# A decoder layer on one core: second Strassen group of the down-projection reordered over two pairs, operand differences emitted earlier, and the last column sums split over two banks

## The chip, the cores and the metric

The kernel runs on one core of a Trainium2 chip. The metric is the device time of one execution in microseconds (us). The profile is of one execution; its own time stands beside its span in the table below. TensorE is called PE in the profile's rows, VectorE DVE, ScalarE ACT, GpSimd POOL, and SyncE, which issues most DMAs here, SP.

## The reference

One layer of a hybrid decoder over 1024 tokens of width 1024: a normalisation, two attention branches, a merge, and then a gated MLP with a short convolution. The change lies wholly in the last product and the final normalisation:

```python
def conv_ffn(xn, w_up, conv_w, conv_b, w_down):
    ...
    gate, val = jnp.split(c, 2, axis=-1)
    return (jax.nn.silu(gate) * val) @ w_down
...
    x = x + conv_ffn(xn, w_up[l], conv_w[l], conv_b[l], w_down[l])
return rmsnorm(x, norm_final_w)
```

`w_down` is 2816 x 1024. Everything is float32.

## The kernel before

Activations lie transposed: 128 channels on the partitions, 1024 tokens along the free axis, in two halves of 512. To keep float32 accuracy on a faster matmul type, each operand is split into a high part (a cast on ScalarE) and a low part (the operand less its high part, a subtraction on VectorE). A product of two operands is then three matmuls: high x high, high x low and low x high. For four blocks of 128 on the inner axis that makes 12 matmuls of 512 columns into one PSUM bank.

**The down-projection, `down()`.** The hidden axis has 22 blocks of 128 rows. The first six (`N1 = 6`) are multiplied plainly. The other sixteen are two groups of eight, and each group is multiplied by Strassen's scheme (in Winograd's form): a weight block row `m` (0 to 3) with row `m + 4` makes a **pair**, the two token halves are the other side, and a pair takes seven products instead of eight:

- P1 = A11 x B11, P2 = A12 x B21, P3 = S4 x B22, P4 = A22 x T4, P5 = S1 x T1, P6 = S2 x T2, P7 = S3 x T3.

A11 and A12 are the raw weight blocks of row `m`, A22 the second of row `m + 4`; S1 to S4 are sums and differences of weight blocks, made on GpSimd with four additions per pair. B11, B21, B22 are blocks of the activations; T1 to T4 are differences of them, made on VectorE by `diffs(k, ...)` with four subtractions for each of four inner blocks `k`.

The result accumulates in one tile `x3` of 8 x 1024 columns in SBUF: VectorE adds each finished bank to it (rows `x<-x,d` and `x<-x,y` in the profile; `d` and `y` are the two kinds of bank, four of each in `psD`).

**Order of the first group.** P1 and P2 of all four pairs come first; then the loop `for m, y in enumerate(ys)` (L1231) runs for each pair P5, P6, P3, P4, P7, that is 60 matmuls. Inside this loop `diffs(k, i)` is emitted four times (L1245, L1250): it makes the differences for the *second* group, each time tied behind one of VectorE's additions by `tc.issue_after`.

**Order of the second group.** The list `more` holds closures that split each activation operand (`prepare(n)` emits the next n). All of B11, B21, T4, T2, T3 and the four result boxes are emitted before the loop over the pairs (L1252); the rest during it. For each pair the loop (L1277) runs P1, P2, then P7 of the pair before (`seventh`), P4, P6. P5 and P3 of the second group come last for all pairs (`fifth`, `third`), because they finish the right half of the tokens, and the final normalisation follows behind them piece by piece. `evac` adds a bank to `x3`, squares the finished sum on ScalarE (L1261), adds the squares up, and multiplies by the norm's weight on ScalarE (L1265).

**Where weights come from.** `plan()` writes a list `wsrc`; `next_w(n)` calls `ahead(n)`, which takes entries from the list and issues loads, GpSimd sums and splits until `n` weight operands are queued. A "second" entry is one pair of the second group: `second_pair` (L138) loads both rows, makes the four sums on GpSimd (L148 to L151), stores S1 and S4 to DRAM (`sd`), and splits A11/A12, S2/S3 and A22. The buffers are few: three raw tiles (`raw`, RAW = 3), two high and two low tiles for A operands (`wh`, `wl`), two of each for S operands (`sh`, `sl`), two for the GpSimd sums (`c`). A cast into a `wh` tile waits until the matmuls that read the operand two before it are done.

**The scheduler.** Tile, the layer under the kernel, places the emitted instructions in one fixed order per engine; each engine then runs strictly in that order. SP's queue is a fixed order too.

**The end, `last_norm`** (L1336). For each piece of tokens `col_sums` (L214) multiplies the squares with a column of ones on PE, block of 128 tokens by block, all into one bank; `rstd_cols` (L221) scales on VectorE (L225) and takes the power on GpSimd (L227); `spread` transposes the result across partitions (L233), and L1361 multiplies and L1362 stores. The right half of the tokens is done in two pieces of 256; the second one ends the program.

Of the kernel before, what the change touches and what calls it, by code (L numbers as in the profile page):

```python
# [10 lines left out]
F32 = mybir.dt.float32  # L11
# [6 lines left out]
P = 128  # L18
D = 1024
# [25 lines left out]
class Trunk:  # L45
    def __init__(self, tc, ins, out):
        self.tc, self.nc = tc, tc.nc
        (self.xT, self.w_in, self.w_br, self.w_mix, self.w_up, self.w_dn,
         self.vecs_d, self.bias_d) = ins
        self.out = out  # L50
        self.uid = 0
        self.stores = []
        self.uw = self.w22 = self.behind = None
        self.pin, self.after = False, None
        self.hs, self.defer, self.late = {}, [], []
# [14 lines left out]
    def ahead(self, n):  # L70
        while len(self.wq) < n and self.wsrc and (self.wsrc[0][1] != "pair" or self.uw):
            src, nk, *eng = self.wsrc.pop(0)
            if nk == "sums":

                self.sums = self.split_pair(*self.sum_pair(src, True, "sl"), 1, 3)
            elif nk == "rest":
                self.sums["A22"] = self.load_w(src[1][:, 4:8], 4)
                self.wq.append(self.sums)
            elif nk == "second":
                self.wq.append(self.second_pair(src, *eng))  # L80
# [57 lines left out]
    def second_pair(self, src, m):  # L138

        nc = self.nc  # L140
        raws = []
        for x in src:
            raws.append(self.tl(self.wp, [P, 8, P], "raw", bufs=RAW))
            nc.sync.dma_start(raws[-1], x)
        g, v = (r.rearrange("p (k a) c -> p a k c", a=2) for r in raws)
        sa, sb = (self.tl(self.sfp[0], [P, 2, 4, P], self.sfp[1]) for _ in range(2))
        tt = nc.gpsimd.tensor_tensor
# [4 lines left out]
        nc.sync.dma_start(self.sd[m], sa.rearrange("p a k c -> p (a k) c"))  # L152
        ops = {}
        for pool, h, l, x, names in ((self.wp, "wh", "wl", g, ("A11", "A12")), (self.uw, "sh", "sl", sb, ("S2", "S3")), (self.wp, "wh", "wl", v[:, 1:2], ("A22",))):
            hi = self.tl(pool, [P, len(names), 4, P], h, F32R)
            lo = self.tl(pool, [P, len(names), 4, P], l, F32R)
            nc.scalar.copy(hi, x)
            nc.vector.tensor_tensor(lo, x, hi.bitcast(F32), ALU.subtract)
            for i, name in enumerate(names):
                ops[name] = hi[:, i], lo[:, i]  # L160
        return ops
# [59 lines left out]
    def rstd_cols(self, ssq_ps, n, width):  # L221
# [3 lines left out]
        nc.vector.tensor_scalar(ms[:, :n], ssq_ps[:, :n], 1.0 / width, EPS, ALU.mult, ALU.add)  # L225
# [52 lines left out]
    def plan(self):  # L278
# [28 lines left out]
        src += [((self.w_dn[m, :, N2:, :], self.w_dn[m + 4, :, N2:, :]), "second", m) for m in range(4)]  # L307
# [800 lines left out]
    def down(self):  # L1108

        nc, tc = self.nc, self.tc  # L1110
        with ExitStack() as ctx:
# [118 lines left out]
            for m, y in enumerate(ys):  # L1230
# [6 lines left out]
                tt(col(m, 1), col(m, 1), y, ALU.add)  # L1237
# [6 lines left out]
                if m in (1, 2):  # L1244
                    diffs(2 * m - 1, i)  # L1245
# [3 lines left out]
                if m < 2:  # L1249
                    diffs(2 * m, i)  # L1250
            prepare(24)
# [3 lines left out]
            def evac(ps, m, hf, a=0, b=H2, last=False):  # L1255
# [5 lines left out]
                nc.scalar.activation(sq, x, AF.Square)  # L1261
# [3 lines left out]
                nc.scalar.mul(x, x, self.vecs[:, C_NO + m:C_NO + m + 1])  # L1265
                return sq

            ys, ws = [], []

# [5 lines left out]
            for m in range(4):  # L1275
                w = self.next_w()
                ws.append(w)  # L1277
# [6 lines left out]
                if m:  # L1284
                    seventh(m - 1)
                ps = bank(0)
                self.product(ps, w["A22"], "2T4")
                tt(col(m + 4, 0), col(m + 4, 0), ps, ALU.subtract)
                self.product(y, w["S2"], "2T2", first=False, skip=True)
                tt(col(m, 1), col(m, 1), y, ALU.add)  # L1290
                prepare(4)
            seventh(3)
# [26 lines left out]
            for a, b in ((0, q), (q, H2)):  # L1319
# [4 lines left out]
                sqs = [box[1][:, a:b], third(2, ws[2], p[0], a, b, True)]  # L1324
                if not a:
                    step()
                sqs.append(third(3, ws[3], p[1], a, b, True))
# [8 lines left out]
    def last_norm(self, psD, sqs, x3, t0, a, b, pieces):  # L1336
# [4 lines left out]
        def sums():  # L1341
            ssq = self.tl(psD, [P, H2], "d")
            self.col_sums(ssq, sqs, n, 0)
# [85 lines left out]
```

## Time and profile before

| | |
|---|---|
| time, median of 3 runs | 1343.12 us (1343.10 to 1344.14) |
| the profiled execution's own time | 1343.35 us |
| its span | 1341.1 us |
| PE busy | 1321.7 us (99%) |
| VectorE busy | 1065.8 us (79%) |
| ScalarE busy | 621.7 us (46%) |
| GpSimd busy | 495.6 us (37%) |
| granted PE clock, mean | 0.995 |
| the first group's pairs (P5 to P7) | from 1190.08 us |
| the second group's first product | from 1244.90 us |
| the last large matmul | ends near 1330.2 us |

Rows of the timeline give the start, the duration, the engine, the line of the kernel, the operation, the output and inputs with their shapes, how many instructions were merged, and in brackets how long the engine had been idle and what ended the wait. A row's duration is a little longer than the distance to the next start where instructions overlap: a VectorE addition of 512 columns shows 0.68 but the next one starts 0.60 later, and matmuls of 512 columns start every 0.227 us while each shows 0.39. A row merged from several instructions gives the sum.

### The profile page before, as it was taken

The numbers are of one execution on the slowest core, as the hardware profiler recorded it, in microseconds if no ns is written. First come the engines' busy times: TensorE is split into PE (matmuls) and PEld (weight loads), VectorE is DVE, ScalarE is ACT, GpSimd is POOL, SyncE is SP. The second block draws the span as 40 slices with busy tenths as digits, with TensorE's granted clock in tenths as the row PEclk, the third lists the DMA queues.
The fourth block names the chain that finished last, engine by engine and source line by source line (L and its number), as shares of the span: only waits on it lengthen the run. The fifth ranks groups of instructions, "written<-read, shape, count | busy, mean of one in ns | idle before, by whom it ended". The sixth has DMA issues, their size and how long they took to land.

```text
span 1341.1 us, 17306 instructions
## 1 busy us (share of the span) xinstructions
PE 1321.7 (99%) x6264; PEld 1097.4 (82%) x6264; DVE 1065.8 (79%) x1603; ACT 621.7 (46%) x1019; POOL 495.6 (37%) x365
## 2 busy tenths in 40 slices
PE   7999999999999999999999999999999999999997
PEld 6888888888888778878888888888888888888787
DVE  8847775289889876465678999999999987869975
ACT  8432232276667665333454444334444434323443
POOL 0336552000102124641446555655556510224412
PEclk9999999999999999999999999999999999999998
DMA  6423443966553235334423222222222239562333
GB/s 258 148 104 150 149 157 141 254 174 188 143 138 130 93 121 200 138 110 157 141 96 108 65 93 90 83 81 77 95 79 90 75 116 330 202 246 71 113 115 126
DMA packets 63045, 182.64 MB, mean 136 GB/s; under 512 B 6896, under 2 KB 15216, under 8 KB 62960
## 3 DMA queue, kind: packets, MB, share of 16 engines
q1 hardware_dynamic: 51504, 164.13, 37.3%
q10 hardware_dynamic: 11456, 17.41, 3.6%
q8 instruction: 49, 0.80, 0.2%
q14 instruction: 36, 0.29, 0.1%
HBM read 130.66 MB, written 50.86 MB: 135 GB/s over the span
## 4 chain that ended last, share of the span: by engine, by line
PE 86%; DVE 5%; POOL 4%; DMA 2%; issue 2%; ACT 1%; POOLq 0%; SPq 0%; ACTq 0%; DVEq 0%
PE t L920 13%; PE t L919 13%; PE t L918 13%; PE g L210 3%; PE g L211 3%; PE g L212 3%; PE t L912 3%; PE sc L634 3%; PE y L1157 2%; PE d L1157 2%; PE sc L212 2%; PE sc L210 2%; PE sc L211 2%; DMA gr<-gd 2%; PE d L918 2%
## 5 line engine op out<-in xcount | busy, mean ns | idle before, releaser
L1087 ACT ACTIVATE c<-us,vecs 128x512 f32<-128x512 f32 x80 | 61.3, 781 | 132.3 <-POOL us L1081 128.3
L1089 DVE SCALAR_TENSOR_TENSOR c<-us,vecs,c 128x512 f32<-128x512 f32 x160 | 110.4, 747 | 8.6 <-ACT c L1087 8.5
L1081 POOL TENSOR_TENSOR us<-us,rstd 128x1024 f32<-128x1024 f32 x38 | 99.6, 2642 | 4.5 <-DVE us L467 2.4
L128 DVE TENSOR_TENSOR sl<-sf,sh 128x1024 fp32r<-128x1024 f32 x62 | 87.6, 1416 | 11.5 <-ACT sh L127 11.5
L127 ACT CAST sh<-sf 128x1024 fp32r<-128x1024 f32 x62 | 63.4, 1048 | 60.4 <-PE t L919 44.0
L177 DVE TENSOR_TENSOR wl<-raw,wh 128x1024 fp32r<-128x1024 f32 (+2 forms) x46 | 57.7, 1255 | 30.2 <-ACT wh L175 18.9
L128 DVE TENSOR_TENSOR wl<-raw,wh 128x1024 fp32r<-128x1024 f32 (+1 forms) x35 | 75.9, 2169 | 3.7 <-ACT wh L127 3.6
L103 POOL TENSOR_TENSOR sf<-rv 128x512 f32<-128x512 f32 x30 | 41.3, 1377 | 100.9 <-DVE sl L128 57.8
L175 ACT CAST wh<-raw 128x1024 fp32r<-128x1024 f32 (+2 forms) x46 | 46.0, 1001 | 62.6 <-PE sc L211 30.5
L210 PE MATMUL g<-xh,wh 128*128 128x512 f32 x176 | 70.7, 402 | 0.1
L212 PE MATMUL g<-xh,wl 128*128 128x512 f32 x176 | 70.4, 400 | 0.0
L211 PE MATMUL g<-xl,wh 128*128 128x512 f32 x176 | 70.3, 400 | 0.0
L108 POOL TENSOR_TENSOR sf<-raw,rv 128x512 f32<-128x512 f32 x30 | 40.7, 1356 | 65.4 <-DVE sl L128 65.4
L617 POOL MEMSET aT<- 128x128 f32 x32 | 6.1, 205 | 151.5 <-PE t L663 63.2
L638 DVE CUSTOM_DVE_ANT_0 L<-sc,bias 128x128 f32<-128x128 f32 (+7 forms) x64 | 47.7, 751 | 17.0 <-PE sc L634 13.7
L639 ACT ACTIVATE L<-L,sm 128x128 f32<-128x128 f32 (+7 forms) x64 | 49.6, 778 | 20.0 <-DVE sm L638 13.5
L792 POOL TENSOR_TENSOR gr<-gr,rstd 128x1024 f32<-128x1024 f32 x16 | 40.4, 2533 | 41.2 <-DMA gr<-gd 40.9
L1091 ACT ACTIVATE c<-c 128x512 f32<-128x512 f32 x40 | 24.0, 600 | 60.7 <-DVE c L1089 60.7
L128 DVE TENSOR_TENSOR wl<-rv,wh 128x512 fp32r<-128x512 f32 x30 | 49.2, 1640 | 3.5 <-ACT wh L127 3.5
L634 PE MATMUL sc<-u,u 128*128 128x512 f32 (+2 forms) x192 | 49.7, 358 | 0.0
L212 PE MATMUL sc<-mh,wl 128*128 128x512 f32 x126 | 49.1, 390 | 0.3 <-DVE wl L177 0.3
L227 POOL TENSOR_TENSOR rs<-ms,mhalf 128x8 f32<-128x8 f32 (+2 forms) x9 | 13.6, 1517 | 96.5 <-DVE ms L225 85.9
(522 smaller groups left out, 4429.6 us busy)
## 6 DMA issues: line engine op xcount, KB each, us to landing
u<-qd SPq DMA_DIRECT2D x72, 256.0 KB, 6.0
raw<-in_w_in SPq DMA_DIRECT2D x25, 512.0 KB, 4.1
raw<-in_w_up SPq DMA_DIRECT2D x23, 512.0 KB, 3.5
hr<-hd SPq DMA_DIRECT2D x46, 256.0 KB, 5.2
hd<-c SPq DMA_DIRECT2D x22, 512.0 KB, 2.6
rv<-in_w_up SPq DMA_DIRECT2D x21, 512.0 KB, 3.5
raw<-in_w_down SPq DMA_DIRECT2D x19, 512.0 KB, 4.1
gr<-gd SPq DMA_DIRECT2D x16, 512.0 KB, 3.5
```

Of the source, the lines that this page charges most:

```text
L127: i = nc.scalar.copy(hi, src)
L128: j = nc.vector.tensor_tensor(lo, src, hi.bitcast(F32), ALU.subtract)
L210: nc.tensor.matmul(ps, wh[:, kc + o, :], ah, start=first and n == 0, stop=False)
L211: nc.tensor.matmul(ps, wh[:, kc + o, :], al, start=False, stop=False)
L212: nc.tensor.matmul(ps, wl[:, kc + o, :], ah, start=False, stop=last and n == len(kcs) - 1)
L634: nc.tensor.matmul(sc[:, lo + n0:lo + n1], qs, k[c][part][:, n0:n1], start=part == 0, stop=part == 1)
L918: nc.tensor.matmul(ps, ah[:, k, :], bh, start=first and n == 0, stop=False, skip_group_check=skip)
L919: nc.tensor.matmul(ps, ah[:, k, :], bl, start=False, stop=False, skip_group_check=skip)
L920: i = nc.tensor.matmul(ps, al[:, k, :], bh, start=False, stop=last and n == len(ks) - 1, skip_group_check=skip)
L1081: (nc.vector if j == 0 else nc.gpsimd).tensor_tensor(u[:, 2:], u[:, 2:], self.rstd, ALU.mult)
L1087: nc.scalar.activation(c, u[:, o + 2:o + 2 + H2], AF.Identity, bias=self.vecs[:, C_CB + m:C_CB + m + 1], scale=col(m, 2))
L1089: nc.vector.scalar_tensor_tensor(c, u[:, o + k:o + k + H2], col(m, k), c, ALU.mult, ALU.add)
```

## The change

Five things are changed, all in `down()` and what it calls.

1. `second_pair` is divided. `upper` loads the row `m` and splits A11/A12; `lower` loads the row `m + 4`, makes the GpSimd sums, stores S1/S4 and splits A22 and then S2/S3 (before: S2/S3, then A22). The list now has upper 0, upper 1, lower 0, lower 1, upper 2, lower 2, upper 3, lower 3.
2. The second group's products come in an order written out by hand: P1 and P2 of pairs 0 and 1, then P4 and P6 of pair 0, P4 of pair 1, P7 of pair 0, P6 of pair 1, P1 and P2 of pair 2, and so on. Three weight operands are kept queued instead of two (`next_w(3)`).
3. The four `diffs` are emitted in pair 0 (three of them) and pair 1 (one) of the first group; before, in pairs 0, 1, 1 and 2. The number of subtractions is unchanged.
4. Between the first 12 and the next 12 prepared operands, `ahead(3)` emits the loads and splits of the first entries.
5. At the end, the multiplication by the norm's weight of the two last products is issued after both squares, and the column sums of a piece of 256 tokens go to two banks (one per block of 128), the squares in the outer loop; VectorE then scales two columns with two instructions.

```diff
         for x in (col(m, 1), col(m + 4, 1)):
             tt(x, x, ps, ALU.add)
         self.product(y, w["S2"], "T2", first=False, skip=True)
-        tt(col(m, 1), col(m, 1), y, ALU.add)
+        i = tt(col(m, 1), col(m, 1), y, ALU.add)
+        if m < 2:
+            diffs(3 * m, i)
...
-        if m in (1, 2):
-            diffs(2 * m - 1, i)
+        if m == 0:
+            diffs(1, i)
...
-        if m < 2:
-            diffs(2 * m, i)
-    prepare(24)
+        if m == 0:
+            diffs(2, i)
+    prepare(12)
+    self.ahead(3)
+    prepare(12)
...
-src += [((self.w_dn[m, :, N2:, :], self.w_dn[m + 4, :, N2:, :]), "second", m) for m in range(4)]
+for ms in ((0, 1), (2,), (3,)):
+    src += [(self.w_dn[m, :, N2:, :], "upper") for m in ms]
+    src += [(self.w_dn[m + 4, :, N2:, :], "lower", m) for m in ms]
...
+for f, m in ((first, 0), (first, 1), (fourth, 0), (sixth, 0), (fourth, 1), (seventh, 0), (sixth, 1), (first, 2), (seventh, 1),
+             (fourth, 2), (sixth, 2), (first, 3), (seventh, 2), (fourth, 3), (sixth, 3), (seventh, 3)):
+    f(m)
+    if f is sixth:
+        prepare(4)
...
-                nc.scalar.mul(x, x, self.vecs[:, C_NO + m:C_NO + m + 1])
-                return sq
+                weigh = lambda: nc.scalar.mul(x, x, self.vecs[:, C_NO + m:C_NO + m + 1])
+                if last:
+                    return sq, weigh
+                weigh()
...
+                with tc.issue_after(self.square.ins):
+                    for _, weigh in ends:
+                        weigh()
...
     def sums():
-        ssq = self.tl(psD, [P, H2], "d")
-        self.col_sums(ssq, sqs, n, 0)
+        if n == NB // 2:
+            ssq = self.tl(psD, [P, H2], "d")
+            self.col_sums(ssq, sqs, n, 0)
+            box.append(self.rstd_cols([ssq[:, :n]], n, D))
+            return
+        ssq = [self.tl(psD, [P, H2], t)[:, 0:1] for t in "dy"]
+        for k, sq in enumerate(sqs):
+            for i, x in enumerate(ssq):
+                nc.tensor.matmul(x, sq[:, i * P:(i + 1) * P], self.ones, start=k == 0, stop=k == len(sqs) - 1)
         box.append(self.rstd_cols(ssq, n, D))
```

**Three places in the engines' orders.** The first is VectorE's order in pair 0 of the first group; `x` rows are additions into the result, `h<-h` rows the four subtractions of `diffs`, `sl` and `wl` rows low halves of weights (`sl_10522` is S1/S2 and `sl_10526` S3/S4 of pair 1). Before:

```order
L1237 TENSOR_TENSOR x_9784<-x_9784,y_10299 128x512
L128 TENSOR_TENSOR sl_10522<-c_10515,sh_10521 128x1024
L1240 TENSOR_TENSOR x_9784<-x_9784,d_10561 128x512
L1243 TENSOR_TENSOR x_9784<-x_9784,d_10575 128x512
L1248 TENSOR_TENSOR x_9784<-x_9784,y_10299 128x512 x2
L128 TENSOR_TENSOR sl_10526<-c_10516,sh_10525 128x1024
L1203 TENSOR_TENSOR h_1810_10495<-h_1810_10495 128x512
```

Now:

```order
L1250 TENSOR_TENSOR x_9784<-x_9784,y_10299 128x512
L1216 TENSOR_TENSOR h_1810_10495<-h_1810_10495 128x512
L130 TENSOR_TENSOR sl_10522<-c_10515,sh_10521 128x1024
L1217 TENSOR_TENSOR h_1810_10495<-h_1811_10496,h_1810_10495 128x512
L1255 TENSOR_TENSOR x_9784<-x_9784,d_10565 128x512
L1218 TENSOR_TENSOR h_1811_10496<-h_1811_10496,h_1810_10495 128x512
L1219 TENSOR_TENSOR h_1811_10496<-h_1811_10496 128x512
L1258 TENSOR_TENSOR x_9784<-x_9784,d_10579 128x512
L1216 TENSOR_TENSOR h_1812_10499<-h_1812_10499 128x512
```

The subtractions stand between pair 0's additions now, where they stood behind all of them. In the same way all 16 subtractions stand ahead of S3/S4 of pair 2 (`sl_10630`) now, where seven of them did before.

The second place is ScalarE's order at the start of the second group. `h<-h` rows cast T operands into high halves (the last ones, with `h_1810` as source a second time, are T1); `wh` of 1024 columns is A11/A12 of a pair, `wh` of 512 columns A22, `sh` S2/S3. Before (`wh_10822` is A22 of pair 0, `sh_10991` S2/S3 of pair 1, `wh_10987` A11/A12 of pair 1):

```order
L157 CAST wh_10822<-raw_10805 128x512
L831 CAST h_1893_10957<-h_1817_10508 128x512
L831 CAST h_1894_10960<-h_1810_10495 128x512
L831 CAST h_1895_10963<-h_1812_10499 128x512
L831 CAST h_1896_10966<-h_1814_10503 128x512
L157 CAST sh_10991<-c_10981 128x1024
L831 CAST h_1897_10969<-h_1816_10507 128x512
L831 CAST h_1915_11056<-h_1810_10495 128x512
L831 CAST h_1916_11059<-h_1812_10499 128x512
L157 CAST wh_10987<-raw_10976 128x1024
```

Now (`wh_10933` is A11/A12 of pair 1, `sh_11025` S2/S3 of pair 1, `wh_10946` A22 of pair 0):

```order
L143 CAST wh_10933<-raw_10931 128x1024
L844 CAST h_1896_10963<-h_1817_10508 128x512
L844 CAST h_1897_10966<-h_1810_10495 128x512
L844 CAST h_1898_10969<-h_1812_10499 128x512
L844 CAST h_1899_10972<-h_1814_10503 128x512
L844 CAST h_1900_10975<-h_1816_10507 128x512
L844 CAST h_1920_11093<-h_1810_10495 128x512
L143 CAST sh_11025<-c_11015 128x1024
L844 CAST h_1921_11096<-h_1812_10499 128x512
L143 CAST wh_10946<-raw_10937 128x512
```

A11/A12 of pair 1 and A22 of pair 0 have changed places, and A22 of pair 0 now stands behind S2/S3 of pair 1.

The third place is VectorE's order at the same point, the low half of S2/S3 of pair 0 (`sl_10819` before, `sl_10951` now), which is the last reader of the GpSimd tile `c` that pair 1's sums are written into. Before:

```order
L832 TENSOR_TENSOR h_1871_10898<-hr_10896,h_1871_10898 128x512
L1237 TENSOR_TENSOR x_9784<-x_9784,y_10468 128x512
L158 TENSOR_TENSOR sl_10819<-c_10808,sh_10818 128x1024
L832 TENSOR_TENSOR h_1873_10903<-hr_10901,h_1873_10903 128x512
L1240 TENSOR_TENSOR x_9784<-x_9784,d_10854 128x512
```

Now (`wl_10934` is A11/A12 of pair 1, `wl_10947` A22 of pair 0; the six `h` rows are T2 and the first two of T3):

```order
L144 TENSOR_TENSOR wl_10934<-raw_10931,wh_10933 128x1024
L1263 TENSOR_TENSOR x_9784<-x_9784,y_10468 128x512 x2
L144 TENSOR_TENSOR sl_10951<-c_10940,sh_10950 128x1024
L845 TENSOR_TENSOR h_1893_10954<-h_1811_10496,h_1893_10954 128x512
L845 TENSOR_TENSOR h_1894_10957<-h_1813_10500,h_1894_10957 128x512
L845 TENSOR_TENSOR h_1895_10960<-h_1815_10504,h_1895_10960 128x512
L845 TENSOR_TENSOR h_1896_10963<-h_1817_10508,h_1896_10963 128x512
L845 TENSOR_TENSOR h_1897_10966<-h_1810_10495,h_1897_10966 128x512
L845 TENSOR_TENSOR h_1898_10969<-h_1812_10499,h_1898_10969 128x512
L144 TENSOR_TENSOR wl_10947<-raw_10937,wh_10946 128x512
```

It stands behind pair 3's last additions of the first group now, where it stood behind the second of them. On SP's queue the row `m + 4` of pair 0 is now third, behind A11/A12 of pair 1 (before, second), and the first reload of `sd` stands ahead of the four `hr<-hd` loads instead of behind them.

More of the change, by code (lines that the diff above doesn't have):

```diff
@@ L54, in __init__ @@
         self.pin, self.after = False, None
-        self.hs, self.defer, self.late = {}, [], []
+        self.hs, self.defer, self.late, self.upper_raw = {}, [], [], []
     def name(self, s):
@@ L78, in ahead @@
                 self.wq.append(self.sums)
-            elif nk == "second":
-                self.wq.append(self.second_pair(src, *eng))
+            elif nk == "upper":
+                self.wq.append(self.upper(src))
+            elif nk == "lower":
+                self.wq.append(self.lower(src, *eng))
             elif nk == "idle":
@@ L151, in second_pair @@
         tt(sa[:, 1], g[:, 1], sb[:, 0], ALU.subtract)
[L152 to L161, printed above, removed]
+        self.nc.sync.dma_start(self.sd[m], sa.rearrange("p a k c -> p (a k) c"))
+        return {**self.halves(self.wp, "wh", "wl", v[:, 1:2], ("A22",)), **self.halves(self.uw, "sh", "sl", sb, ("S2", "S3"))}
     def load_raw(self, src, nk):
```

63 lines of the change are left out of this document (37 added, 26 removed).

## Prediction

> **What bounds the kernel now.** First the page: busy times, then the chain that ended last.
>
> ```profile
> PE 1321.7 (99%) x6264; PEld 1097.4 (82%) x6264; DVE 1065.8 (79%) x1603; ACT 621.7 (46%) x1019; POOL 495.6 (37%) x365
> PE 86%; DVE 5%; POOL 4%; DMA 2%; issue 2%; ACT 1%; POOLq 0%; SPq 0%; ACTq 0%; DVEq 0%
> ```
>
> PE has almost no idle time, and the number of large matmuls doesn't change. The change can win only where PE waits, and after its last matmul. So I read PE's timeline over the second group.
>
> ```profile
> 1244.90 1.98 PE L912 MATMUL y<-h,wh 128*128 128x512 f32 x8
> 1246.71 1.07 PE L914 MATMUL y<-h,wl 128*128 128x512 f32 x4
> ...
> 1250.34 0.39 PE L918 MATMUL d<-h,wh 128*128 128x512 f32 x1
> 1251.04 0.50 PE L919 MATMUL d<-h,wh 128*128 128x512 f32 x1 [0.31 <-DVE h L832]
> ...
> 1253.45 0.39 PE L920 MATMUL d<-h,wl 128*128 128x512 f32 x1
> 1255.70 2.52 PE L912 MATMUL y<-h,wh 128*128 128x512 f32 x8 [1.86 <-ACT wh L157]
> 1258.02 0.63 PE L918 MATMUL d<-h,wh 128*128 128x512 f32 x1
> 1258.80 2.03 PE L914 MATMUL y<-h,wl 128*128 128x512 f32 x4
> ...
> 1262.06 0.39 PE L918 MATMUL y<-h,sh 128*128 128x512 f32 x1
> ```
>
> Undisturbed, eight matmuls take 1246.71 - 1244.90 = 1.81 us, 0.227 each. Between 1250.34 and 1262.06 stand 31 matmuls, worth 7.03 us; they took 11.72. So **4.7 us** are lost here. P4 of pair 0 waits for the low half of T4 (0.47), P1 of pair 1 for its weights (2.02), their low half for VectorE (0.55), and 1.65 remain for slow matmuls. One window of a microsecond shows those (the last three figures are the granted clock, the DMA share and GB/s), where three matmuls fit instead of four and more:
>
> ```profile
> 1259.00:1260.00 1.00, 1.00 (x3) 0.81 (x4) 1.00 (x2) 0.00 (x0) 0.00 (x0) 0.50 0.26 37
> ```
>
> Why were pair 1's weights late? ScalarE's cast of them stood behind casts of T operands, which waited for VectorE:
>
> ```profile
> 1253.48 1.22 ACT L831 CAST h<-h 128x512 fp32r<-128x512 f32 x2 [3.23 <-DVE h L832]
> 1254.61 1.04 ACT L157 CAST wh<-raw 128x1024 fp32r<-128x1024 f32 x1
> ```
>
> And VectorE was late because the 16 subtractions of `diffs` began only at 1206.22, after idle time that nothing used:
>
> ```profile
> 1193.00 1.28 DVE L1235 TENSOR_TENSOR x<-x,d 128x512 f32<-128x512 f32 x2 [0.64 <-PE d L920]
> 1195.72 0.69 DVE L1237 TENSOR_TENSOR x<-x,y 128x512 f32<-128x512 f32 x1 [1.44 <-PE y L920]
> ...
> 1201.16 0.69 DVE L1243 TENSOR_TENSOR x<-x,d 128x512 f32<-128x512 f32 x1 [2.03 <-PE d L920]
> ...
> 1205.08 1.22 DVE L128 TENSOR_TENSOR sl<-c,sh 128x1024 fp32r<-128x1024 f32 x1
> 1206.22 0.69 DVE L1203 TENSOR_TENSOR h<-h 128x512 f32<-128x512 f32 x1
> 1206.82 1.78 DVE L128 TENSOR_TENSOR wl<-raw,wh 128x512 fp32r<-128x512 f32 x1
> ```
>
> The number in brackets is the idle time ahead of a row. Behind 1206.22 VectorE's timeline shows no idle time for 58 us.
>
> **Step 1, the products' order: -4.7.** With P1, P2 of pair 1 behind those of pair 0, PE works from 1244.90 to 1255.78 (48 x 0.227) on operands that were ready (pair 1's cast can begin once P4 of the first group's pair 3 has read the tile before, at 1244.90 - 12 x 0.227 = 1242.2). T4 is wanted at 1255.78 instead of 1250.34. All three waits go. What is late next is step 3.
>
> **Step 2, diffs in pairs 0 and 1: +0.2.** The data are there: the `h<-hd` loads are issued from 1186.9, and none takes over 9.8, so the first pair of tiles waits until 1196.7 at most, against 1196.3.
>
> ```profile
> L1196 SPq DMA_DIRECT2D h<-hd x8: 327/416/664, 1186.9 to 1190.6; - x8
> DMA to landing us min/median/max: 4.1/7.5/9.8
> ```
>
> But all 16 now precede S3/S4 of pair 2, whose low half P3 needs at its third matmul. Pair 0 begins here:
>
> ```profile
> 1190.08 0.39 PE L918 MATMUL d<-h,sh 128*128 128x512 f32 x1
> ```
>
> That gives 1190.08 + (120 + 24 + 2) x 0.227 = 1223.2. VectorE's queue from 1193.0 to there: 14 additions, 16 subtractions and 2 A22 halves at 0.60, 4 halves of 1024 columns at 1.13 (starts of 1205.08 and 1206.22), together 23.7; 2.2 of forced waiting for PE, for the banks of 1195.72 and 1201.16; and six GpSimd instructions beside it. The row at 1206.82, quoted above, lasted 1.1 longer than its neighbour's 0.69, while GpSimd added; where additions from PSUM stand between, the cost falls to 0.5 (1.19 against 0.68):
>
> ```profile
> 1233.77 0.68 DVE L1205 TENSOR_TENSOR h<-h,h 128x512 f32<-128x512 f32 x1
> ...
> 1234.97 1.19 DVE L1206 TENSOR_TENSOR h<-h 128x512 f32<-128x512 f32 x1
> ```
>
> So the half is ready between 1221.9 and 1225.5; at 0.7 each it is 1223.2. I take 0.2 us, the bounds are 0 and 2.3.
>
> **Step 3, A22 of pair 0: +1.1, and +0.4 of slow clock.** P4 of pair 0 needs A22's low half at 1255.78 + 0.45 = 1256.2. The orders make a chain: low half of S2/S3 of pair 0 (VectorE) frees the `c` tile; GpSimd makes S2, S3 of pair 1 in it; ScalarE casts them; only then does it cast A22 of pair 0. VectorE begins at 1233.77 (the row above starts when S3/S4 of the last pair is done): 12 splits and 7 additions at 0.60, two halves of 1.13, that is 13.7, to 1247.4; four GpSimd instructions cost 1.0 (as seen in that stretch before) to 4.4; I take 2.4, so 1249.8. Then GpSimd at its slowed rate:
>
> ```profile
> 1245.20 1.74 POOL L150 TENSOR_TENSOR c<-raw,raw 128x512 f32<-128x512 f32 x1
> 1245.71 3.47 DVE L832 TENSOR_TENSOR h<-hr,h 128x512 fp32r<-128x512 f32 x2
> ```
>
> Two of them until 1253.3, ScalarE's casts of 1.04, 0.61 and 0.61 (rows above) until 1255.5. VectorE meanwhile does six T splits, three at 1.70 and three at 0.60, until 1256.7, then A22's half until 1257.3. PE waits 1.1. With the ends of the port cost the wait is 0 (1248.4) or 3.1 (1251.8). For the clock I take 0.4, between nothing (after the gap of 0.47 matmuls kept nearly full pace) and 1.65. Pair 1's A22 follows at 1262.1, wanted at 1262.8.
>
> The Trainium skill ("SBUF — State Buffer", SBUF: two separate sides) calls the port pair of VectorE and GpSimd an exclusive lock held for the whole instruction, and frees VectorE instructions with one SBUF input from it; the trace agrees: 0.60 for `x` rows, 1.70 for `h` rows. By its rule each GpSimd instruction would cost up to its whole undisturbed length, 1.3 in the rows of that engine, instead of 1.1, and step 3 would be some 0.6 longer. Its page "TensorE: Matmul & The Clock Gate" (Why this matters for your kernels) lets the clock fall after gaps of about 3 us; the trace shows 0.50 after a gap of 2.02, so the measurement decides. By the page the 0.4 would be nothing and the sum 1338.6.
>
> **Step 4, the end: -1.2.** The chain of waits near its end, with the two squares (`hr`), the weighing between them and the sums:
>
> ```profile
> 1330.51 0.42 ACT hr L1261
> 1330.95 0.51 ACT x L1265
> 1331.46 0.31 ACT hr L1261
> 1331.82 1.45 PE d L218 x8
> ```
>
> With both squares first, the second ends at 1331.37 instead of 1331.78 (VectorE's two additions stand back to back ahead of the first, so its sum is there). Eight PE rows still follow the last square, because the blocks come one after the other; now four do. At full clock one takes 0.117 (the twelve of the earlier piece, below, in 1.40); in the last stretch 0.18 (1.45 for eight).
>
> ```profile
> 1324.14 1.40 PE L218 MATMUL d<-ones,hr 128*128 128x1 f32 x12
> ```
>
> At full clock the sums are done at 1331.4 + 4 x 0.117 and a last latency, 1332.0, instead of 1333.27, a gain of 1.3; at the slow rate, where the second square's rows also queue, 0.8. I take 1.2, since the four rows then begin ahead of 1332, earlier than most of the eight did. The second VectorE scaling (0.16) begins when the other bank's is done; that is inside the bounds. The weighings moved back hide behind the sums: the scaling that reads them comes behind GpSimd's power.
>
> Edits without a price: SP's new order delays the row `m + 4` of pair 0 to about 1227.2 and 1231.4, hidden by the `c` tile's release at 1233.8; without that cover each us later costs one in step 3. The sums of the earlier 256 piece had 0.29 of slack on GpSimd.
>
> **Sum.** -4.7 + 0.2 + 1.1 + 0.4 - 1.2 = -4.2. Against the profiled execution's 1343.35 (2.25 outside its span, unchanged): 1339.15; that execution lies 0.2 above the median of the runs, so **1339.0**.
>
> **Rivals.**
> - *No wait is left.* If GpSimd costs VectorE the lower price, steps 2 and 3 are nothing: 1343.35 - 5.9 = 1337.4. For it: VectorE has idle time around 1228 to catch up; against it: 1.70 per instruction in every stretch where both work from SBUF. 0.25.
> - *The wait moves to P4 of pair 0 nearly whole.* Step 3 at its upper end with the slow clock: 3.1 + 1.65 + 0.2 given back, 1342.4. For it: the chain is strictly in order; against it, additions from PSUM stand among the splits. 0.22.
> - *Slower: the queues starve pair 3.* Row `m + 4` of pair 2 is loaded after A22 of pair 0 is split (1257.3), lands in 4.2, its four sums at 1.74 end near 1268.9, and SP passes the store, the next load and the `sd` reload before the four `hr` loads; at about 0.4 for each issue that is until 1271.7. DMA issues before, with the median us to landing:
>
> ```profile
> raw<-in_w_down SPq DMA_DIRECT2D x16, 512.0 KB, 4.2
> h<-hd SPq DMA_DIRECT2D x8, 512.0 KB, 7.5
> hr<-hd SPq DMA_DIRECT2D x15, 256.0 KB, 4.3
> ```
>
>  They land by 1276.0. On ScalarE the cast of pair 3's A11/A12 stands behind their four casts, at about 1278; P1 of pair 3, 168 matmuls behind 1244.90 and 1.7 later by steps 2 and 3, wants it at 1284.7. That slack of 6.7 hides it. It makes the kernel slower than before once the loads are 6.7 + 4.2 = 11 us late; at 13 late it is 6.3 + 1.65 more: 1347.0. Against it: none of the loads above took 10. 0.05.
>
> **How the numbers follow.** My forecast (1338.4 to 1341.0) has 0.46; 0.02 is for what I don't see. 0.2% (2.7 us) is about what a measurement of this kernel can tell from no change: faster means below 1340.4. That takes nine tenths of the forecast and all of the first rival: 0.67. Same is the rest of the forecast and most of the second rival, 0.28; slower 0.05. The range reaches from the first rival, with step 4 at its best, to the second: 1337.0 to 1342.4.
>
> **What would show it.** Step 1: no PE wait from 1250 to 1255, and a granted clock of 1.00. Step 2: PE in the first group's pair 2 waiting at most some tenths for an `sl` row. Step 3: a wait of about 1 us for a 512-column `wl` or `wh` as P4 of pair 0 begins, and the GpSimd sums of pair 1 starting just behind an `sl` row of VectorE. Step 4: two neighbouring squares, then four PE rows, and GpSimd's power 1.2 earlier, counted from the last large matmul. I am wrong if VectorE is late at another place, or if the first group's P3 waits for more than a microsecond.

## The result and the profile after

The changed kernel is slower, by 0.4%: 1349.87 us median (1344.4 to 1352.45, 13 runs) against 1344.14 (1341.89 to 1346.46, 13 runs), a ratio of 1.0039 with an interval of 1.0028 to 1.005. The prediction had 1339.0, in a range of 1337.0 to 1342.4.

The page of the changed kernel, busy times and the chain that ended last. It answers to the two lines of before that open the prediction:

```profile
PE 1322.4 (98%) x6264; PEld 1097.7 (81%) x6264; DVE 1067.0 (79%) x1605; ACT 621.1 (46%) x1019; POOL 494.7 (37%) x365
PE 85%; DVE 6%; POOL 4%; DMA 2%; issue 2%; ACT 1%; POOLq 0%; SPq 0%; ACTq 0%; DVEq 0%
```

PE's busy time is the same within 0.7 us and its share of the span has fallen by a point: PE stands idle, and VectorE has one per cent more of the chain. What PE waits for in the two groups and the end (us in total, times, longest), from the waits of PE in the changed kernel:

```profile
PE y L931 <- DVE x L1307: 5.8, 1, 5.8
PE y L931 <- DVE x L1250: 1.5, 1, 1.5
...
PE d L933 <- DVE wl L144: 0.9, 1, 0.9
```

Three single waits. The last one was predicted (A22's low half at P4 of pair 0). The other two were not, and both are of one kind: the **first matmul of a P7** waits for an addition of VectorE (`x<-x,y`). PE's timeline at these places, start first:

```profile
1215.71 0.39 PE L933 MATMUL d<-h,wl 128*128 128x512 f32 x1
1217.63 0.50 PE L931 MATMUL y<-h,sh 128*128 128x512 f32 x1 [1.54 <-DVE x L1250]
1217.97 0.39 PE L932 MATMUL y<-h,sh 128*128 128x512 f32 x1
...
1258.81 0.39 PE L932 MATMUL d<-h,wh 128*128 128x512 f32 x1
1260.10 0.50 PE L933 MATMUL d<-h,wl 128*128 128x512 f32 x1 [0.90 <-DVE wl L144]
1260.43 0.40 PE L931 MATMUL d<-h,wh 128*128 128x512 f32 x1
...
1267.71 0.39 PE L933 MATMUL d<-h,wl 128*128 128x512 f32 x1
1273.91 0.80 PE L931 MATMUL y<-h,sh 128*128 128x512 f32 x1 [5.81 <-DVE x L1307]
1274.50 0.63 PE L932 MATMUL y<-h,sh 128*128 128x512 f32 x1
...
1280.05 0.42 PE L933 MATMUL y<-h,sl 128*128 128x512 f32 x1
```

Starts should be 0.227 apart. At P7 of pair 1 (first group) 1.69 are lost and 0.11 in the next step, together 1.80; at P4 of pair 0 1.06 and 0.10, 1.16; at P7 of pair 0 (second group) 1273.91 - 1267.71 - 0.227 = 5.97. From there to 1280.05 stand 14 steps, worth 3.18, in 6.14: 2.96 more go to the half clock. That is **11.9 us** lost, against 4.69 in the kernel before, and 1.22 gained at the end (below): +6.0. From the first addition of the first group to the span's end the changed kernel takes 1348.2 - 1194.38 = 153.82, the kernel before 1341.1 - 1193.00 = 148.10: +5.7. The ledger closes within 0.3. (The two spans differ by 7.1; the other 1.4 lies ahead of that addition.)

Why is P7 tied to an addition? P1, P6 and P7 of a pair accumulate in the same `y` bank. Behind P6, VectorE adds the bank to column half (m, 1); P7 may write into it only when that has been read. P6 of pair 0 ends about 1265.2, but VectorE's queue stands so (timeline of VectorE, then of GpSimd, changed kernel):

```profile
1265.29 2.89 DVE L845 TENSOR_TENSOR h<-h,h 128x512 fp32r<-128x512 f32 x2
1268.11 1.75 DVE L1281 TENSOR_TENSOR hr<-hr,hr 128x512 f32<-128x512 f32 x1
1269.78 2.28 DVE L144 TENSOR_TENSOR wl<-raw,wh 128x1024 fp32r<-128x1024 f32 x1
1271.98 0.68 DVE L1303 TENSOR_TENSOR x<-x,d 128x512 f32<-128x512 f32 x1
1272.58 0.68 DVE L845 TENSOR_TENSOR h<-h,h 128x512 fp32r<-128x512 f32 x1
1273.18 0.68 DVE L1307 TENSOR_TENSOR x<-x,y 128x512 f32<-128x512 f32 x1
```

```profile
1264.45 1.48 POOL L164 TENSOR_TENSOR c<-raw 128x512 f32<-128x512 f32 x1 [6.76 <-DMA raw<-in_w_down]
...
1269.38 1.59 POOL L167 TENSOR_TENSOR c<-raw,c 128x512 f32<-128x512 f32 x1
```

Three splits of T1 (emitted behind P6), the sum of squares and the low half of pair 2's weights stand ahead of the addition L1307; in e4, below, most of them stand behind it and nobody waits for them. No row has idle time ahead of it. The rows with two inputs in SBUF last longer while GpSimd makes pair 2's sums (e8, below, shows them without). The addition starts nearly 8 us after P6's end.

The new order doesn't give P7 of pair 0 less cover on PE than it had. The loop of the kernel before emits P1 and P2 of pair 1, 24 matmuls, between P6 and P7 of pair 0, but PE ran them in another order: all of P1 and seven matmuls of P2 came ahead of P6, and five stood between P6 and P7. The end of P6, the start of P7 and VectorE's addition in the kernel before:

```profile
1264.57 0.39 PE L920 MATMUL y<-h,sl 128*128 128x512 f32 x1
...
1265.92 0.40 PE L918 MATMUL y<-h,sh 128*128 128x512 f32 x1
```

```profile
1264.99 0.69 DVE L1290 TENSOR_TENSOR x<-x,y 128x512 f32<-128x512 f32 x1 [0.91 <-PE y L920]
```

There VectorE had been idle for 0.91 and read the bank as soon as P6 was done; PE lost nothing. Three splits of T1 stood ahead of the addition there too, but they took 1.88 and were over before P6 ended, for PE came late, after the waits of step 1. In the new order P4 of pair 1 (12 matmuls, 2.7 us) stands between P6 and P7, and that is not enough for a VectorE so far behind.

The first group has the same knot. There P3 and P4 stand between P6 and P7, as before, but VectorE has the early subtractions ahead (changed kernel, VectorE):

```profile
1215.16 0.68 DVE L1219 TENSOR_TENSOR h<-h 128x512 f32<-128x512 f32 x1
1215.76 1.21 DVE L130 TENSOR_TENSOR sl<-c,sh 128x1024 fp32r<-128x1024 f32 x1
1216.90 0.68 DVE L1250 TENSOR_TENSOR x<-x,y 128x512 f32<-128x512 f32 x1
```

P6's addition of pair 1 begins at 1216.90, and PE was ready for P7 at 1215.94.

Two windows of the changed kernel (PE, PEld, DVE, ACT and POOL busy with instructions in brackets, granted clock, DMA share, GB/s) show the stretch that step 1 freed, and the one behind the long wait:

```profile
1246.00:1259.00 13.00, 13.00 (x59) 10.59 (x57) 13.00 (x15) 6.68 (x12) 6.29 (x4) 1.00 0.04 15
...
1274.00:1280.00 6.00, 6.00 (x14) 4.71 (x15) 2.22 (x4) 0.94 (x1) 1.27 (x1) 0.50 0.67 226
```

### The profile page after: what moved, and what is told of

It reads as the page before. It is cut to its first block, busy times and chain, and to the rows that moved or that the text cites. A ratio compares the mean times of both kernels' runs of the same rounds, so it can differ in the third digit from the quotient of the medians.

```text
span 1348.2 us, 17306 instructions
## 1 busy us (share of the span) xinstructions
PE 1322.4 (98%) x6264; PEld 1097.7 (81%) x6264; DVE 1067.0 (79%) x1605; ACT 621.1 (46%) x1019; POOL 494.7 (37%) x365
## 4 chain that ended last, share of the span: by engine, by line
PE 85%; DVE 6%; POOL 4%; DMA 2%; issue 2%; ACT 1%; POOLq 0%; SPq 0%; ACTq 0%; DVEq 0%
PE t L933 13%; PE t L932 13%; PE t L931 13%; PE g L218 3%; PE g L219 3%; PE g L220 3%; PE t L925 3%; PE sc L647 3%; PE y L1170 2%; PE d L1170 2%; PE sc L220 2%; PE sc L218 2%; PE sc L219 2%; DMA gr<-gd 2%; PE d L931 2%; PE d L933 2%
```

## The experiments

In the table, "wait 1" is P7 of pair 1 in the first group, "wait 2" P4 of pair 0 and "wait 3" P7 of pair 0 in the second group, in us from PE's waits in each profile. "Stage" is the profiled span less the start of VectorE's first `x<-x,d` pair of the first group. "Half clock" is its length: twice the sum of (1 - granted clock) over windows of 1 us from 1205 to 1310. Each ratio is to the kernel before on the same chip, whose medians there lay between 1344.1 and 1344.6. Where PE waits 0.3 or more for something else in the second group, the last column says where.

| kernel | median us | ratio, 95% | wait 1 / 2 / 3 | half clock | stage | other waits |
|---|---|---|---|---|---|---|
| before | 1344.14 | | 0 / 0.3 / 0 | 3.4 | 148.1 | 1.9 at P1 of pair 1 |
| changed | 1349.87 | 1.0039, 1.0028-1.005 | 1.5 / 0.9 / 5.8 | 6.8 | 153.8 | |
| e1_end_alone | 1343.16 | 0.9987, 0.9979-0.9996 | 0 / 0.3 / 0 | 0 | 146.3 | 1.9 at P1 of pair 1, 0.8 behind it |
| e2_sums_as_before | 1347.93 | 1.0027, 1.0017-1.0036 | 0 / 0 / 5.9 | 6.8 | 151.7 | 1.1 at P4 of pair 1 |
| e3_sums_alone | 1347.64 | 1.0019, 1.001-1.0027 | 1.9 / 0 / 0 | 3.4 | 150.3 | 3.5 at P1 of pair 1 |
| e4_addition_first | 1342.23 | 0.9983, 0.9974-0.9991 | 1.5 / 0.9 / 0.9 | 0 | 145.9 | |
| e5_first_sums_before | 1344.5 | 1.0002, 0.9988-1.0016 | 0 / 1.5 / 1.5 | 0 | 146.6 | 0.4 at P6 of pair 0 |
| e6_splits_behind | 1346.12 | 1.0009, 0.9999-1.002 | 2.0 / 1.1 / 2.5 | 6.8 | 151.7 | |
| e7_p7_later | 1347.74 | 1.0022, 1.0011-1.0032 | 1.5 / 0.9 / 3.1 | 0 | 148.2 | |
| e8_no_sums_pair2 | 1345.46 | 1.0008, 0.9997-1.0019 | 1.5 / 0.9 / 2.1 | 3.4 | 148.8 | |
| e9_two_and_two | 1340.23 | 0.9968, 0.9955-0.9981 | 0 / 1.1 / 0 | 0 | 144.1 | 0.4 at P7 of pair 1 |
| e10_two_p7_later | 1340.88 | 0.9972, 0.9961-0.9982 | 0 / 1.2 / 0 | 0 | 145.4 | 1.1 at P6 of pair 2 |
| e11_addition_first_again | 1342.35 | 0.9989, 0.998-0.9999 | 1.4 / 1.0 / 0.9 | 0 | 145.8 | |
| e12_two_and_two_alone | 1346.14 | 1.0008, 0.9999-1.0017 | 0 / 0 / 0 | 6.8 | 149.6 | 3.5 at P1 of pair 1 |

The **theory**: the loss is PE's wait at P7 for VectorE's reading of the `y` bank, above all at pair 0 of the second group, and the half clock behind it. **Rivals**: the early subtractions alone; GpSimd's sums alone, which lengthen VectorE's rows; a loss at the end; or that VectorE simply has too much to do there, in whatever order.

### The edits apart: e1, e2, e3

e1 is the kernel before with point 5 of the change alone: the weighings behind both squares, and the column sums in two banks.

> The kernel before with the edits at the end alone (squares ahead of the weighings, one bank per block of the last sums). Theory (the loss sits in waits of P7 for VectorE's addition, and the end gained 1.2): 1344.1 - 1.2 = 1342.9 (1342.6 to 1343.3), the distance from the last large matmul to GpSimd's power 2.2 instead of 3.4. Rival (the end lost as well, hidden in the sum): 1344 or more, distance 3.4 or more.

Measured: 1343.16, 1.2 below before; the last large matmul starts at 1331.82 and GpSimd's power at 1334.02, 2.20 apart. In the changed kernel the timeline of the end has the same distance:

```profile
1338.35 0.28 PE L933 MATMUL d<-h,sl 128*128 128x256 f32 x1
...
1338.75 0.79 ACT L1279 ACTIVATE hr<-x 128x256 f32<-128x256 f32 x2 [1.72 <-DVE x L1276]
...
1339.91 0.36 PE L1380 MATMUL y<-ones,hr 128*128 128x1 f32 x2
...
1340.55 0.70 POOL L238 TENSOR_TENSOR rs<-ms,mhalf 128x2 f32<-128x2 f32 x1 [2.44 <-DVE ms L236]
```

The two squares stand together, and four PE rows follow the second (1339.54): the rows at 1339.68 and 1339.91, two in each. Before, the distance was 1333.53 - 1330.11 = 3.42. The end gains; that rival falls.

e2 is the changed kernel with the old conditions for the subtractions:

```diff
-                if m < 2:
-                    diffs(3 * m, i)
...
-                if m == 0:
-                    diffs(1, i)
+                if m in (1, 2):
+                    diffs(2 * m - 1, i)
...
-                if m == 0:
+                if m < 2:
-                    diffs(2, i)
+                    diffs(2 * m, i)
```

> The changed kernel with the operand subtractions back at their places of before (behind pairs 0, 1, 1, 2). Theory (P7 waits for the addition behind P6; the early subtractions cost only the 1.7 in the first group and help the second): the 1.7 at P7 of pair 1 of the first group goes, VectorE comes later into the second group by about 3 to 5, P7 of pair 0 still waits 5 or more, and P4 of pair 0 waits longer; 1350 to 1354. Rival (the early subtractions alone put VectorE behind): 1343 or less, and no wait at P7 of pair 0 of the second group.

Measured: 1347.93, under the range. PE's waits in e2:

```profile
PE y L931 <- DVE x L1305: 5.9, 1, 5.9
PE d L931 <- ACT wh L143: 1.1, 1, 1.1
```

Wait 1 is gone, wait 3 is the same 5.9. So the early subtractions don't make the long wait, and that rival falls. But the second group starts no worse, against what I had expected: P4 of pair 0 doesn't wait at all, and P4 of pair 1 waits 1.1 for its weights' cast. The scheduler's order had changed at a place that the edit does not touch: ScalarE casts A22 of pair 0 ahead of S2/S3 of pair 1 here, and four splits stand ahead of A22's low half on VectorE, not six. They took 0.6 each (four in 2.48 from 1254.67), where the six in the changed kernel took 6.99 from 1252.45, beside GpSimd's sums for pair 1. In e2 it was GpSimd that was held up: its second sum lasted 6.34 (from 1254.98), against 1.52 in the changed kernel, the cast of S2/S3 waited 6.0 for the sums, and A22 of pair 1 stood behind that cast.

e3 is the kernel before with the early subtractions alone.

> The kernel before with the subtractions early (all four in pairs 0 and 1) and nothing else changed. Theory: 1.7 lost at P7 of pair 1 in the first group, 2 to 4.7 won back between P2 of pair 0 and P7 of the second group because T4's halves are split earlier; 1341.0 to 1344.0. Rival (the early subtractions alone make the loss): 1348 to 1350, with a wait of some 5 us in the second group.

Measured: 1347.64, between the two. PE's waits in e3:

```profile
PE y L912 <- ACT wh L157: 3.5, 1, 3.5
PE y L918 <- DVE x L1237: 1.9, 1, 1.9
```

The 1.9 is wait 1, as the theory has it. What I expected to be won back in the second group was not: the wait for pair 1's weights grew from 1.9 to 3.5. e12 takes that up.

### The long wait by doses: e4, e6, e7, e8

e4 holds the splits of T1 and the low half of pair 2's weights behind the addition on VectorE; no instruction is added or left out.

```diff
-                ws.append(self.next_w(3))
+                ws.append(self.next_w(3 if m else 2))
...
-                tt(col(m, 1), col(m, 1), ys[m], ALU.add)
+                return tt(col(m, 1), col(m, 1), ys[m], ALU.add)
...
-                f(m)
+                i = f(m)
                 if f is sixth:
-                    prepare(4)
+                    with tc.issue_after(i.ins):
+                        if m == 0:
+                            self.ahead(2)
+                        prepare(4)
```

> The changed kernel, but on VectorE the addition behind P6 of pair 0 of the second group stands ahead of the four splits of T1 and of the low half of pair 2's A11/A12 (both kept behind it). No instruction is left out. Theory (P7 of pair 0 waits for that addition, and the half clock after the gap is its echo): the addition ends at about 1268 instead of 1273.9, the wait of 5.8 falls under 1, the 2.9 of slow clock go too: 1340.5 to 1342.5. Rival (VectorE has too much to do at this place, in whatever order): the wait moves to P1 of pair 2 or P4 of pair 1 with 3 us or more, 1346 or more.

Measured: 1342.23, and 1342.35 when it was run again as e11. VectorE in e4:

```profile
1266.40 1.67 DVE L1281 TENSOR_TENSOR hr<-hr,hr 128x512 f32<-128x512 f32 x1 [0.70 <-ACT hr L1279]
1267.98 0.68 DVE L1303 TENSOR_TENSOR x<-x,d 128x512 f32<-128x512 f32 x1
1268.58 0.68 DVE L1307 TENSOR_TENSOR x<-x,y 128x512 f32<-128x512 f32 x1
1269.18 1.21 DVE L144 TENSOR_TENSOR wl<-raw,wh 128x1024 fp32r<-128x1024 f32 x1
1270.31 3.58 DVE L845 TENSOR_TENSOR h<-h,h 128x512 fp32r<-128x512 f32 x4
```

The addition starts at 1268.58 instead of 1273.18, the wait is 0.9 instead of 5.8, and the half clock is gone. The same work behind the addition makes no new wait: VectorE had not too much to do here, it did it in the wrong order.

e6 keeps only the splits behind (the `tc.issue_after` around `prepare(4)`, without the change to `next_w`).

> The changed kernel with only the four splits of T1 kept behind the addition of P6 of pair 0; the low half of pair 2's A11/A12 stays ahead of it. A part of e4's dose. Theory: three splits fewer ahead (2.89 + 0.60), so the addition stands near 1269.8, PE waits about 2.4 at P7 of pair 0 instead of 5.8: 1344.5 to 1347.0, between the changed kernel and e4. Rival (it is not the queue of VectorE ahead of the addition): as the changed kernel, 1349 to 1351, or as e4.

e7 exchanges two entries of the order:

```diff
-... (fourth, 1), (seventh, 0), (sixth, 1), (first, 2), ...
+... (fourth, 1), (sixth, 1), (seventh, 0), (first, 2), ...
```

> The changed kernel with P7 of pair 0 moved on PE behind P6 of pair 1, so that 24 matmuls stand between P6 and P7 of pair 0 as in the kernel before. Theory: the addition ends at 1273.9 as in the changed kernel, PE comes to P7 2.7 later, the wait is about 3.1 instead of 5.8: 1346.0 to 1347.5. Rival (the distance on PE is the cause, VectorE's queue is not): no wait at P7, 1341 to 1342.

e8 leaves GpSimd's four sums for pair 2 out:

```diff
+        if m == 2:
+            self.nc.sync.dma_start(self.sd[m], g.rearrange("p a k c -> p k a c"))
+            return {**self.halves(self.wp, "wh", "wl", v[:, 1:2], ("A22",)), **self.halves(self.uw, "sh", "sl", g, ("S2", "S3"))}
```

> The changed kernel without GpSimd's four sums for pair 2 of the second group (S2, S3 are taken from the raw blocks, and raw blocks are stored in place of S1, S4). Theory (VectorE's own order makes it late; the shared port only adds to it): the five VectorE rows between 1265.3 and 1272 fall back to 0.60 and 1.14, 3.7 us less, the wait at P7 of pair 0 falls from 5.8 to about 2: 1344.5 to 1346.5. Rival (GpSimd alone makes VectorE late): the wait goes altogether, 1341 to 1342.

Measured, wait 3 in each, one fence for each kernel (e6, e7, e8):

```profile
PE y L931 <- DVE x L1307: 2.5, 1, 2.5
```

```profile
PE y L931 <- DVE x L1307: 3.1, 1, 3.1
```

```profile
PE y L934 <- DVE x L1310: 2.1, 1, 2.1
```

Expected were 2.4, 3.1 and about 2. Each dose takes from the wait what it takes from VectorE's queue, or adds to the cover on PE, and no more. (e7's expectation calls 24 matmuls the distance of before; that holds for the later pairs, for pair 0 it was five.) In e8 the addition starts at 1268.88, with two T1 splits in 1.28 instead of 2.89 and the weights' low half in 1.21 instead of 2.28 (VectorE in e8):

```profile
1264.74 1.28 DVE L848 TENSOR_TENSOR h<-h,h 128x512 fp32r<-128x512 f32 x2
1265.95 0.67 DVE L1284 TENSOR_TENSOR hr<-hr,hr 128x512 f32<-128x512 f32 x1
1266.55 1.21 DVE L144 TENSOR_TENSOR wl<-raw,wh 128x1024 fp32r<-128x1024 f32 x1
```

So without GpSimd's sums the wait is 3.7 shorter, and with the addition first (e4) 4.9. The two overlap, since the rows that GpSimd lengthens are those that stand ahead of the addition: they can't be added up. Neither rival (distance alone, GpSimd alone) takes the whole wait away. e6's profile differs from the changed kernel's at another place too: wait 1 is 2.0 and brings a half clock of its own. The medians of e6 and e8 lie in their ranges, that of e7 0.2 above. e7's profiled execution (span 1343.0) lies 2.9 under its median: it kept the full clock over the 3.1, with a mean clock of 0.998, where ten of the other eleven executions had 0.995 to 0.997.

### Better versions: e5, e9, e10

e5 puts the edits of e2 and e4 together.

> The addition ahead (as in e4_addition_first) and the subtractions back at their places of before. Theory (the early subtractions bring VectorE no earlier into the second group, since its splits there begin only when PE has freed the T operands of the first group near 1237; they cost only the wait at P7 of pair 1): e4's time less 1.5 to 2, 1340.0 to 1341.0; no PE wait in the first group. Rival (the early subtractions do help the second group): the second group loses what the first gains, 1342 or more.

Measured: 1344.5, in a wide spread (1340.74 to 1350.07). The rival has it: wait 1 goes, and waits 2 and 3 grow to 1.5 each (e4: 0.9 each), with 0.4 at P6 of pair 0. In this profile the second group loses about what the first gains. That the early subtractions as such help the second group is not shown by it: e2 has the same orders up to wait 2 and no wait there. Its four splits took 2.48 beside GpSimd's sums, e5's took 5.78. And the profile is of a fast execution, 3.2 under the median; what the slower ones lose is not on record.

e9 is e4 with 8 subtractions in pair 0 and 8 in pair 1, so that the addition behind P6 of pair 1 stands ahead of the second eight:

```diff
                 if m < 2:
-                    diffs(3 * m, i)
+                    diffs(2 * m, i)
...
-                if m == 0:
-                    diffs(2, i)
+                if m == 1:
+                    diffs(3, i)
```

> As e4_addition_first, but the 16 early subtractions stand 8 in pair 0 and 8 in pair 1 of the first group (behind P6 and P4 of pair 0, behind P6 and P7 of pair 1), so that the addition behind P6 of pair 1 comes ahead of the third and fourth eight-instruction halves. Theory (the wait of 1.5 at P7 of pair 1 is that addition standing behind them): this wait goes, the second group stays as in e4 (0.9 and 0.9), 1340.3 to 1341.5, ahead of both kernels. Rival (some other row holds P7, or the second group loses what the first gains, as in e5): 1342 or more.

Measured: 1340.23 (1338.01 to 1341.47, 5 runs), ahead of both kernels and of e4 (1342.35 as e11, on the same chip). The profile is of the fastest of the five. VectorE in the first group, then PE's waits in e9:

```profile
1208.67 1.27 DVE L1248 TENSOR_TENSOR x<-x,d 128x512 f32<-128x512 f32 x2
1209.87 0.67 DVE L1250 TENSOR_TENSOR x<-x,y 128x512 f32<-128x512 f32 x1
1210.46 0.68 DVE L1216 TENSOR_TENSOR h<-h 128x512 f32<-128x512 f32 x1
```

```profile
PE d L933 <- DVE wl L144: 1.1, 1, 1.1
...
PE y L931 <- DVE x L1307: 0.4, 1, 0.4
```

The addition behind P6 of pair 1 now stands ahead of the third set, wait 1 is gone, and the second group has lost nothing. The 0.4 is at P7 of pair 1 here, not of pair 0.

e10 adds e7's exchange.

> As e9_two_and_two, with P7 of pair 0 of the second group behind P6 of pair 1 on PE as well. Theory: the 0.9 at P7 of pair 0 goes, 0.9 at P4 of pair 0 stays: 1339.5 to 1341.0. Rival (P2 of pair 2 or P7 of pair 1 then waits for an addition in its place): 1341.5 or more.

Measured: 1340.88, in the range, but not ahead of e9: 1.1 now falls on P6 of pair 2, which waits for the addition behind its own P1 in the `y` bank. The knot has moved, though not to a place that the rival named.

> e4_addition_first again, beside the two that build on it: 1342.2 (1341.5 to 1343.0), waits as before.

Measured: 1342.35, in the range.

### The early subtractions in the old order: e12

> The kernel before with the subtractions 8 in pair 0 and 8 in pair 1 (as in e9_two_and_two) and nothing else changed. Theory (the early subtractions as such do no harm; e3 lost 1.9 at P7 of pair 1 and by what PE's lateness moved behind it): no wait in the first group, the second group loses 3 to 4.7 as before between P2 of pair 0 and P7, 1343.0 to 1344.6. Rival (the early subtractions make the second group's start worse, as the 3.5 wait of e3 for the weights' cast seems to say): 1345.5 or more, with that wait at 3 or more and no wait in the first group.

Measured: 1346.14; the rival has it. There is no wait in the first group, and PE waits 3.5 for pair 1's weights. ScalarE in e12:

```profile
1254.97 1.22 ACT L831 CAST h<-h 128x512 fp32r<-128x512 f32 x2 [3.14 <-DVE h L832]
1256.45 1.14 ACT L831 CAST h<-h 128x512 fp32r<-128x512 f32 x2 [0.26 <-ACT h L831]
1257.49 1.56 ACT L157 CAST wh<-raw 128x1024 fp32r<-128x1024 f32 x2
```

The weights' cast starts 62.4 behind the stage's first addition (1257.49 - 1195.07); before, it was 61.6 (1254.61 - 1193.00). It is not earlier, although all subtractions are. ScalarE's order has changed here as well: behind its wait four casts of T operands stand ahead of the weights' cast, where the kernel before had two (its rows of 1253.48 and 1254.61 are in the prediction). The first of them starts 59.9 behind the stage's first addition (1254.97 - 1195.07), before 60.5. So the early subtractions bring this chain forward by 0.6, and the two more casts take that back. They were not what made ScalarE late by microseconds. Three splits beside GpSimd's sums take 5.18 in e12, which is part of it; what else holds the chain was not tried.

## Why the prediction was wrong, point by point

**Step 1, -4.7: this step failed**, in the sentence "All three waits go. What is late next is step 3." The first half came true: from 1246 to 1259 PE runs 13.00 of 13.00 at clock 1.00. The second did not. I looked for operands that come late, and a P7 needs something else as well: that VectorE has read the bank it adds to. In the kernel before that cost nothing, because PE came late to P6 and found VectorE idle. With PE's waits gone, the reading for P7 of pair 0 stood behind splits of T1, a sum of squares and pair 2's weights on VectorE, in rows that GpSimd's sums lengthened, and the 12 matmuls between P6 and P7 did not cover that. The wait is 5.97 and its half clock 2.96, 8.9 us, which the sum has at nothing; with the addition first (e4) the kernel is 7.6 faster than the changed one. The prediction's own sign of being wrong, that VectorE is late at another place, is what came.

The reason that I gave for the late weights, that the subtractions began only at 1206.22, falls as well: e12 has them early and the weights no earlier. The order of the products removes that wait (e2, with the subtractions at their old places, has none at P1 of pair 1), the subtractions do not.

**Step 2, +0.2: it cost 1.8.** The deadline that I worked out, the low half of S3/S4 for P3 of pair 2, did not bind. P7 of pair 1 did, for the same reason as above, with the addition behind the third set of subtractions. e9 shows it: two sets in each pair, and no wait.

**Step 3, +1.1 and +0.4: right**, and by the chain that it names. P4 of pair 0 waited 0.9 by the profile, 1.16 in lost time, 1.1 in e9; GpSimd's sums began at 1252.76, behind the `sl` row, and six splits of together 6.99 stood ahead of A22's low half (6.9 in the prediction). The size is not firm: in e2 and e5, with four splits ahead, the wait was 0 and 1.5. The 0.4 for the clock was not needed there.

**Step 4, -1.2: right**, 1.22 in the changed kernel and 1.2 in e1. A part of it is the clock: in the profile of before it was at half from 1332.33, over the last column sums, in the changed kernel only from 1341.53, behind them.

**The rivals.** The slower one, queues that starve pair 3, had nothing to do with it. With both P7 knots loosened (e9), the stage is 148.10 - 144.09 = 4.0 shorter than before, by the medians on its chip 4.4; the sum was -4.2. In that sense the terms were fair together and one mechanism was missing, at 0.05 for all slower cases.

## What to carry to other kernels

When products move on PE, list for each PSUM bank not only the operands of the next matmul into it, but the reading that must come between two accumulations, and ask two things: how many matmuls cover it, and what stands ahead of it in the reader's queue. Take both from the profile's rows and not from the program's loop, and ask whether the reader was on time only because PE was late. The repair cost nothing here: the short read that frees a bank first, the splits that nobody needs yet behind it.

## What the runs showed of the hardware

The half clock comes in pieces of one length. From 1205 to 1310 its length by the windows is 3.4 (before, e3, e8, and twice in e6) or 6.8 (changed kernel, e2, e12), so a gap that triggers it costs up to 1.7 or 3.4 us beside itself. Waits of 1.54 or less never brought it there. Waits of 1.86 (before), 2.02 and 2.52 (e6), 2.06 (e8), 3.5 (e3, e12) and 5.8 or more (changed kernel, e2) did; 1.88 (e1), 1.94 (e3) and 3.11 (e7) did not.

The length of a wait is not all that counts. In the seven profiles with more than one fall, the falls, and the rises from 1205 to 1310, lie whole multiples of 3.413 us apart (read from windows of 0.05 us): in the kernel before it falls at 1257.24, rises at 1260.65 and falls again at 1332.33, 22 such steps behind the first; in the changed kernel it falls at 1273.27, rises at 1280.10 and falls at 1341.53, 20 steps behind the first. Laid back from these times, every fall from 1205 to 1310 stands at the end of a step in which PE was idle for 1.86 or more. The 3.11 of e7 is cut by such a limit into 1.76 and 1.35 (laid back from its fall at 1338.00), the 1.94 of e3 into 0.95 and 0.99. Only the 1.88 of e1 lies in one step by the same working and brought no fall, so the limit must be close to it. The half clock lasts two steps where PE was still idle as it began (changed kernel, e2, e12). At the end of the kernel shorter waits are enough: the fall of before at 1332.33 comes behind waits of 0.33 and 0.46, with only matmuls of one column between them.

The Trainium skill ("TensorE: Matmul & The Clock Gate", Part 1: The HAM clock gate (the "warmup" mystery)) tells of a free-running window of about 3.4 us; the steps agree with it. It asks for an idle window before the clock falls; here 1.86 was enough, and the measurement decides.

Which of VectorE and GpSimd is held up is not fixed by their orders. e2 and e5 have the same rows at the sums for pair 1; in e2 VectorE's four splits took 2.48 and GpSimd's second sum 6.34, in e5 5.78 and 1.52.

One execution of such a kernel tells little: e5 and e7 spread over 9 and 7 us. Mean clocks of 0.995 and 0.998 differ by about 4 us in 1345 (an estimate, 0.003 of it). Another part lies ahead of all that was changed: the stage of e4 begins at 1194.72, that of e11, the same kernel, at 1197.29. What makes the rest is not shown.
